# A hybrid trunk on one core: block inverses issued in another rhythm beside two projections, one scaling moved to ScalarE, and a gate in one operation

## The chip, the cores and the metric

The kernel runs on one core of one Trainium2 chip. The metric is the device time of one execution in microseconds (us). A core has TensorE (matrix products, PE in the profile; its weight loads are listed as PEld), VectorE (DVE), ScalarE (ACT), GpSimd (POOL), SyncE (SP, which here only issues transfers) and 16 DMA engines. Each engine runs its own instructions in one fixed order and waits by semaphores for the others. PSUM is the small memory that TensorE writes to.

## The reference, cut to what matters

The trunk has two layers over 1024 tokens of width 1024, batch 1: one RWKV-7 layer, one differential attention layer, a gated input embedding after each, and a last norm. The change lies in the first layer:

```
xm = h + dx * mu                          # one mix for each of r, k, v and gate
r, k, v, gate = xm_i @ w_in[i]            # four projections, 1024 x 1024 each
kk = k * k_k / |k * k_k| per head ;  b = kk * a
for t in tokens:                          # 16 heads, a state of 64 x 64 each
    sa    = state @ kk_t
    state = state * w_t - sa b_t^T + v_t k_t^T
    y_t   = state @ r_t
y = groupnorm(y) + bonus
h = h + (y * silu(gate)) @ w_out
```

## The kernel before, in words

**The recurrence in chunks.** The scan over tokens is done in 16 chunks of 64 tokens. Inside a chunk the steps depend on each other through a unit lower triangular matrix of 64 x 64 per head, which has to be inverted. With 16 chunks and 16 heads there are 256 such matrices. They don't depend on the state, so they are inverted ahead of the chain of chunks, and the results lie in the tiles `ti`, which the chain's products `u` read.

**Four quarters.** The inverses are made for four chunks at a time, in quarters 0 to 3, by three generators. They issue a piece of work at each `next` and then `yield`, so that the pieces can be written between other work:

- `inv_pb` (from L507): for each of four chunks it loads `bb` and `kk` and multiplies them on TensorE into two PSUM tiles `pb` (32 products of 64 x 64). Each `pb` times a factor per token, head and chunk (`rn`) goes to a part of the tile `nq` (L531). The PSUM tag "aux" has two buffers, so `pb` of the next chunk can only start when both have been read.
- `inv_diag` (from L534): it transposes the four 32 x 32 blocks on the diagonals of `nq` into `nb` (L542), inverts 32 x 32 triangles for all matrices at once in 31 steps of two VectorE operations each (L558, L560, tiles `tm` and `tb`), and transposes the result into `ea` (L570) and `ti` (L575). The copies `prhs` and `ti` (L574, L578) are ScalarE's.
- `inv_merge` (from L581): it makes the block below the diagonal from the two inverted ones by two rounds of 64 small products (`pg`, then `po`, L593), with ScalarE's copies `pairs` and `prhs` between (L603, L604) and behind.

A quarter's `inv_merge` runs beside the next quarter's `inv_pb` and `inv_diag`; `inv_steps` takes turns between the two generators.

**Where they are written.** The pieces are interleaved with two projections, by calls of `tick`. The v projection is 32 tiles of 24 products of 256 columns (L657 to L661), each tile copied to `vst` on ScalarE and stored to DRAM (L664). The gate projection (`dense_T`, L691) is 16 tiles of 24 products of 512 columns; its `ev_g` makes the sigmoid by a tanh on ScalarE and two VectorE operations (L645, L646). Every product is done in three parts (L75 to L77), high times high, high times low and low times high, from tiles that `split` makes. The gate's own operand `xm` is made during the last v tiles by `make_half` (`xmt` on ScalarE, L228, and VectorE, L229, then a cast and a subtraction on GpSimd). From the 48th `gtick` on everything that is left of the inverses is issued at once, and then the first pieces of `stage1` (transposes `kbt`, products `pm`, `prt`) for the first chunk of the chain.

**What sets the order.** The Tile scheduler takes the program and sets a static order per engine from the dependences and its own estimate of times; what is written earlier goes first where both could start. Only the products in one `turns` list are tied to each other. So an instruction may stand ahead of work that was written before it.

**Names.** A tile's number tells its place: `pb41` is chunk 4, half 1; `nq1`, `nb1`, `ea0`, `ti0` belong to quarters 1, 1, 0, 0; `v17` is column quarter 1 and token block 7 of v; `d360` is the projection with index 3 (gate), tile 6, half 0; `wv...h` and `...l` are high and low parts of weights.

Of the kernel before, what the change touches and what calls it, by code (L numbers as in the profile page):

```python
# [36 lines left out]
@with_exitstack  # L37
def trunk(ctx: ExitStack, tc: tile.TileContext, A, out):
    nc = tc.nc
    V, S, G, T = nc.vector, nc.scalar, nc.gpsimd, nc.tensor  # L40

    cp = ctx.enter_context(tc.tile_pool(name="const", bufs=1, reuse_waits="tile"))
    dp = ctx.enter_context(tc.tile_pool(name="scratch", bufs=1, space=DRAM))
# [26 lines left out]
    def split(hi, lo, src, lo_eng=None):  # L70
        S.activation(hi, src, AF.Copy)
        (lo_eng or G).tensor_tensor(out=lo, in0=src, in1=hi.bitcast(F32), op=ALU.subtract)

    def mm3(ps, ah, al, bh, bl, start, stop):
        T.matmul(ps, lhsT=ah, rhs=bh, start=start, stop=False)  # L75
# [117 lines left out]
    with NB("ab") as ab, NP("psab") as pp:  # L193
# [306 lines left out]
        def inv4(tag, nm):  # L500
            return iv.tile([P, 32, 32], F32, tag=tag, name=nm, bufs=1)

        Y1, Y2 = 3, 2
        nqs = {}
        ivt = []

        def inv_pb(q):  # L507

            nq = iv.tile([P, 4, 2, 4, L], F32, tag="nq", name=f"nq{q}", bufs=1)
            nqs[q] = nq.rearrange("p c h j l -> p (c h j) l")  # L510
            for cc in range(4):
                c = 4 * q + cc
                bb = iv.tile([P, KT, L], F32, tag="bb", name=f"bb{c}", bufs=2)
                kk = iv.tile([P, KT, L], F32, tag="kk", name=f"kk{c}", bufs=2)
                for t, src in ((bb, kb_d), (kk, kkr_d)):
                    for st in range(2):
                        js = slice(4 * st, 4 * st + 4)
                        nc.sync.dma_start(out=t[:, js], in_=src[js, :, c, st].rearrange("j p l -> p j l"))

                pb = [pp.tile([P, 4, L], F32, tag="aux", name=f"pb{c}{h}", bufs=2) for h in range(2)]  # L520
                ms = []
                for p_ in range(4):
                    for st in (1, 0):
                        o = 64 * st
                        for h in (1, 0):
                            hs_ = slice(h * 64, h * 64 + 64)
                            ms.append(T.matmul(pb[h][o:o + 64, p_], lhsT=bb[hs_, 4 * st + p_],
                                               rhs=kk[hs_, 4 * st + p_], start=True, stop=True))
                turns(ms)
                for h in range(2):  # L530
                    V.tensor_tensor(out=nq[:, cc, h], in0=pb[h],  # L531
                                    in1=rn[:, c, h].unsqueeze(2).to_broadcast([P, 4, L]), op=ALU.mult)
                    yield

        def inv_diag(q):

            nqf = nqs[q]
            nb = inv4("nb", f"nb{q}")
            for st in range(2):
                for b in range(2):  # L540
                    r0 = 64 * st + 32 * b
                    V.transpose(nb[r0:r0 + 32],  # L542
                                nqf[r0:r0 + 32, :, 32 * b:32 * b + 32].rearrange("p h t -> p t h"))
                yield
            tb = inv4("tb", f"tb{q}")
            G.memset(tb, 0.0)
            G.memset(tb.rearrange("p a b -> p (a b)")[:, 0::33], 1.0)
            ti = tis[q]
            tm = iv.tile([P, 256], F32, tag="tm", name=f"tm{q}", bufs=1)
            if not ivt:  # L550

                ivt[:] = iv.tile([P, 16, 32], F32, name="prhs"), iv.tile([P, 16, L], F32, name="pairs")
                G.memset(ivt[1], 0.0)
            prhs, pairs = ivt
            for j in range(31):
                w, n = j + 1, 31 - j
                tv = tm[:, 0:n * w].rearrange("p (n w) -> p n w", w=w)
                V.tensor_tensor(out=tv, in0=tb[:, j:j + 1, 0:w].to_broadcast([P, n, w]),  # L558
                                in1=nb[:, j + 1:32, j:j + 1].to_broadcast([P, n, w]), op=ALU.mult)
                V.tensor_tensor(out=tb[:, j + 1:32, 0:w], in0=tb[:, j + 1:32, 0:w], in1=tv, op=ALU.add)  # L560
                if j % 4 == 3:
                    yield
                if j == 28:
                    for st in range(2):
                        o = 64 * st
                        for y in range(2):
                            S.copy(pairs[o + 32 * y:o + 32 * y + 32, :, 32 * y:32 * y + 32],
                                   nqf[o:o + 32, 16 * y:16 * y + 16, 32:64])
            ea = inv4("ea", f"ea{q}")
            V.transpose(ea.rearrange("p h s -> p s h"), tb.rearrange("p t s -> p s t"))  # L570
            for st in range(2):
                o = 64 * st
                for y in range(2):
                    S.copy(prhs[o + 32 * y:o + 32 * y + 32], ea[o:o + 32, 16 * y:16 * y + 16])  # L574
            V.transpose(ti[:, :, 0:32].rearrange("p h t -> p t h"), tb)  # L575
            for st in range(2):
                r = slice(64 * st + 32, 64 * st + 64)
                S.copy(ti[r, :, 32:64], ti[r, :, 0:32])  # L578
                G.memset(ti[r, :, 0:32], 0.0)

        def inv_merge(q):  # L581

# [16 lines left out]
            for st in range(2):  # L599
# [3 lines left out]
                    S.copy(pairs[r, :, 32 * y:32 * y + 32], pg[st][r])  # L603
                    S.copy(prhs[r], ti[o + 32:o + 64, hs_, 32:64])  # L604
                yield
            for _ in range(Y2 + 1):
                yield
            po = products("po")
            yield
# [4 lines left out]
                yield  # L614

        def inv_steps():
            for q in range(5):
                def first():
                    if q < 4:
                        yield from inv_pb(q)  # L620
                        yield from inv_diag(q)
                a, b = first(), inv_merge(q - 1) if q else iter(())
                alive = True
                while alive:
                    alive = False
                    for g in (a, b):
                        if next(g, g) is not g:
                            alive = True
                            yield

        bg = inv_steps()

        due = [0.0]
        TV, TG = 1.0, 2.0

        def tick(n):
            due[0] += n
            while due[0] >= 1.0:
                due[0] -= 1.0
                next(bg, None)  # L640

        def ev_g(j, hf, ps):
            e = ab.tile([P, 512], F32, tag="xmt", name=f"ge{j}{hf}", bufs=3)
            S.activation(e, ps, AF.Tanh, scale=0.5)
            V.tensor_scalar(out=e, in0=e, scalar1=0.5, scalar2=0.5, op0=ALU.mult, op1=ALU.add)  # L645
            V.tensor_tensor(out=e, in0=ps, in1=e, op=ALU.mult)  # L646
            nc.scalar.dma_start(out=sg_d[j, :, half(hf)], in_=e)


        new = [None, None]  # L650
        for q in range(4):
            wv = [wload(f"wv{q}{k2}", A["wv"][q, k2].rearrange("p k c -> p (k c)")) for k2 in range(2)]
# [20 lines left out]
        def gtick():  # L673

            npt[0] += 1
            if npt[0] < 48:
                tick(TG)
            elif npt[0] == 48:
                tick(1000)
                iv_cm.__exit__(None, None, None)  # L680
                cm = early["cm"] = tc.tile_pool(name="early", bufs=1, reuse_waits="tile", side="right")
                e = early["co"] = cm.__enter__()
# [8 lines left out]
        dense_T(3, A["wT"][2], new, ev_g, None, gtick)  # L691
        while first:
            first.pop(0)()

    nslot = [0]

# [119 lines left out]
    with NB("d") as d, NP("psco") as pp:  # L816
# [119 lines left out]
        def d1_pieces(i):  # L936
# [38 lines left out]
            def turn(hf):  # L975
# [6 lines left out]
                for q in range(4):  # L982
                    kt = hf * 4 + q
                    V.scalar_tensor_tensor(out=yg[:, kt], in0=ps[:, q], scalar=vec["ln_b"][:, kt:kt + 1],
                                           in1=yg[:, kt], op0=ALU.add, op1=ALU.mult)
                split(gh[:, hs], gl[:, hs], yg[:, hs], V)

            def mms(hf, k0):
                gh, gl = w["gh"], w["gl"]
# [645 lines left out]
```

## Time and profile before

| | us |
|---|---|
| median of 3 runs | 1830.32 (1828.99 to 1832.56) |
| the profiled execution | 1828.3 |
| its span | 1826.5 |
| TensorE busy | 1684.7 (92%) |
| VectorE busy | 1350.9 (74%) |
| ScalarE busy | 760.4 (42%) |
| GpSimd busy | 634.5 (35%) |

The mean granted TensorE clock of the span is 0.963. The chain that ended last is 51% TensorE and 10% VectorE. These are averages over projections, the recurrence, attention and the embedding; the change touches one stretch, from about 314 to 600 us, so most of what is read below is from there. A waiting engine is shown in the rows by what released it; times are us from the start of the span.

### The profile page before, as it was taken

The numbers are of one execution on the slowest core, as the hardware profiler recorded it, in microseconds if no ns is written. First come the engines' busy times: TensorE is split into PE (matmuls) and PEld (weight loads), VectorE is DVE, ScalarE is ACT, GpSimd is POOL, SyncE is SP. The second block draws the span as 40 slices with busy tenths as digits, with TensorE's granted clock in tenths as the row PEclk, the third lists the DMA queues.
The fourth block names the chain that finished last, engine by engine and source line by source line (L and its number), as shares of the span: only waits on it lengthen the run. The fifth ranks groups of instructions, "written<-read, shape, count | busy, mean of one in ns | idle before, by whom it ended". The sixth has DMA issues, their size and how long they took to land.

```text
span 1826.5 us, 30473 instructions
## 1 busy us (share of the span) xinstructions
PE 1684.7 (92%) x11320; PEld 1397.6 (77%) x11320; DVE 1350.9 (74%) x3083; ACT 760.4 (42%) x1594; POOL 634.5 (35%) x705
## 2 busy tenths in 40 slices
PE   6899999898897988898899999899999999999998
PEld 5677778887676877777678878788888888777786
DVE  7878954698994687666766747887877878856665
ACT  6566543346344332223333434444444444544332
POOL 4436644224324355455310333323323323311200
PEclk9999999998998989999999999999999999999999
DMA  7125444434225534444243411101101101431121
GB/s 267 41 61 166 129 106 109 125 102 119 73 67 186 186 127 127 122 129 131 97 172 128 132 51 39 54 7 56 56 7 56 53 10 56 154 99 34 58 93 69
DMA packets 164401, 175.97 MB, mean 96 GB/s; under 512 B 74845, under 2 KB 127837, under 8 KB 164254
## 3 DMA queue, kind: packets, MB, share of 16 engines
q1 hardware_dynamic: 161950, 169.84, 30.2%
q10 hardware_dynamic: 2304, 4.20, 0.6%
q8 instruction: 89, 1.46, 0.4%
q14 instruction: 58, 0.48, 0.1%
HBM read 124.19 MB, written 49.81 MB: 95 GB/s over the span
## 4 chain that ended last, share of the span: by engine, by line
PE 51%; DVE 10%; ACT 2%; issue 1%; DMA 0%; POOL 0%; ACTq 0%; DVEq 0%
PE qkv L75 6%; PE qkv L76 6%; PE qkv L77 6%; PE av L1359 3%; PE sc L1319 2%; PE sc L1320 2%; PE fg L75 2%; PE fg L76 2%; PE fg L77 2%; PE op L75 2%; PE op L77 2%; PE op L76 2%; PE do L75 1%; PE pg L76 1%; PE pg L77 1%; PE do L76 1%
## 5 line engine op out<-in xcount | busy, mean ns | idle before, releaser
L1329 ACT ACTIVATE e<-sc,mx 128x256 f32<-128x256 f32 (+7 forms) x128 | 94.0, 738 | 111.0 <-DVE mx L1326 60.0
L1273 POOL TENSOR_TENSOR rp<-rp,rq 128x128 f32<-128x128 f32 x64 | 34.8, 543 | 237.6 <-DVE rq L1268 189.7
L1359 PE MATMUL av<-vh,aT 128*128 128x128 f32 x576 | 81.1, 280 | 6.3 <-DVE aT L1355 6.3
L1359 PEld LDWEIGHTS av<-vh,aT 128*128 128x128 f32 x576 | 75.6, 195 | 12.8 <-DVE aT L1355 8.9
L1325 DVE TENSOR_REDUCE mxs<-sc 128x1 f32<-128x128 f32 (+6 forms) x112 | 74.2, 682 | 0.5
L1319 PE MATMUL sc<-k,q 128*128 128x512 f32 (+2 forms) x192 | 71.5, 379 | 2.2 <-ACT e L1329 2.2
L229 DVE SCALAR_TENSOR_TENSOR xmt<-hT,cB,xmt 128x512 f32<-128x512 f32 x64 | 63.5, 1012 | 6.6 <-ACT xmt L228 6.3
L1320 PE MATMUL sc<-k,q 128*128 128x512 f32 (+2 forms) x192 | 64.8, 348 | 0.0
L1361 ACT ACTIVATE o<-av,r 128x128 f32<-128x128 f32 x64 | 23.5, 367 | 88.4 <-PE av L1359 88.4
L875 POOL TENSOR_TENSOR spl<-state,plast 64x256 f32<-64x256 f32 x60 | 41.4, 690 | 49.6 <-DVE state L910 42.7
L1341 DVE SCALAR_TENSOR_TENSOR e<-e,r,e 128x128 f32<-128x128 f32 (+3 forms) x64 | 56.5, 883 | 1.2
L560 DVE TENSOR_TENSOR tb<-tb,tm 128x31 f32<-128x31 f32 (+15 forms) x124 | 53.9, 435 | 3.6
L558 DVE TENSOR_TENSOR tm<-tb,nb 128x31 f32<-128x31 f32 (+15 forms) x124 | 53.9, 434 | 3.6
L188 DVE TENSOR_TENSOR m<-pm,mmask 128x512 f32<-128x512 f32 x64 | 41.1, 682 | 20.0 <-PE pm L185 19.7
L1301 POOL CAST q<-q 64x128 fp32r<-64x128 f32 x128 | 38.5, 302 | 49.4 <-PE sc L1320 45.6
L1267 DVE TENSOR_TENSOR rp<-qkv,rc 128x256 f32<-128x256 f32 x64 | 27.1, 423 | 38.3 <-PE qkv L77 30.1
L1292 POOL CAST k<-k 64x256 fp32r<-64x256 f32 x64 | 26.1, 408 | 83.7 <-ACT k L1290 82.5
L185 PE MATMUL pm<-kkr,kb 64*128 64x128 f32 x512 | 50.8, 307 | 3.1 <-ACT kbn L176 2.2
L1355 DVE COPY aT<-at 128x512 f32<-128x512 f32 (+2 forms) x96 | 52.0, 550 | 1.1 <-PE at L1353 0.4
L185 PEld LDWEIGHTS pm<-kkr,kb 64*128 64x128 f32 x512 | 40.4, 203 | 12.9 <-issue 6.0
L1353 PE MATMUL at<-ident,e 128*128 128x128 f32 x288 | 47.4, 277 | 2.8 <-DVE e L1341 2.3
L923 ACT COPY y<-xy 64x512 f32<-64x512 f32 x32 | 18.6, 580 | 71.4 <-PE xy L916 71.0
(1180 smaller groups left out, 6001.5 us busy)
## 6 DMA issues: line engine op xcount, KB each, us to landing
pp_d<-ppo SPq DMA_DIRECT2D x32, 256.0 KB, 2.3
kb_d<-kb SPq DMA_DIRECT2D x16, 512.0 KB, 2.6
kkr<-kkr_d SPq DMA_DIRECT2D x32, 256.0 KB, 3.2
kb<-kb_d SPq DMA_DIRECT2D x32, 256.0 KB, 3.3
x<-in_x SPq DMA_DIRECT2D x8, 512.0 KB, 5.5
kkr_d<-ep SPq DMA_DIRECT2D x16, 256.0 KB, 2.6
kkr_d<-rt SPq DMA_DIRECT2D x16, 256.0 KB, 2.6
bb<-kb_d SPq DMA_DIRECT2D x32, 128.0 KB, 2.6
```

The costliest lines, as they stand in the source:

```text
L75: T.matmul(ps, lhsT=ah, rhs=bh, start=start, stop=False)
L76: T.matmul(ps, lhsT=ah, rhs=bl, start=False, stop=False)
L77: T.matmul(ps, lhsT=al, rhs=bh, start=False, stop=stop)
L185: ms.append(T.matmul(pm[h][:, p_], lhsT=kb[hs, p_], rhs=kkr[hs, p_], start=True, stop=True))
L229: V.scalar_tensor_tensor(out=t, in0=hT[:, kt, half(hf)], scalar=cB[:, g, kt:kt + 1], in1=t, op0=ALU.mult, op1=ALU.add)
L558: V.tensor_tensor(out=tv, in0=tb[:, j:j + 1, 0:w].to_broadcast([P, n, w]), in1=nb[:, j + 1:32, j:j + 1].to_broadcast([P, n, w]), op=ALU.mult)
L1319: T.matmul(ps[:, b0:b1], lhsT=q1[:, m, ts_], rhs=k1[:, m, b0:b1], start=True, stop=False)
L1320: T.matmul(ps[:, b0:b1], lhsT=q0[i % 2][:, m], rhs=k2[:, b0:b1], start=False, stop=True)
L1325: V.tensor_reduce(out=seed, in_=ps[:, 0:n - P], axis=AX.X, op=ALU.min)
L1329: S.activation(e[:, 0:n], ps[:, 0:n], AF.Exp, scale=-1.0, bias=mx, accum_out=l_[:, m:m + 1])
L1341: V.scalar_tensor_tensor(out=es[0][:, 0:n], in0=es[1][:, 0:n], scalar=r[:, 1:2], in1=es[0][:, 0:n], op0=ALU.mult, op1=ALU.add)
L1359: T.matmul(po, lhsT=aT[kb // 4][:, kb % 4], rhs=c["vh"][:, kb], start=(kb == 0), stop=(kb == i))
```

## The change

- All four engines are reached through a small wrapper. While `pin` is set for TensorE, from the first v tile to the end of the gate projection and the first `stage1` pieces, each of its instructions keeps the order in which it is written; the scheduler still orders the other engines. (The wrapper is line 50 of the changed kernel, and all its instructions bear that line.)
- The scaling of `pb` by `rn` goes from two VectorE operations of 128 x 256 per chunk to eight ScalarE operations of 128 x 64, each with its factor per partition as a pointer operand.
- The four transposes into `nb`, each over 32 partitions, become one over all 128 and two over 32 (the first writes something into the two ranges that the other two then overwrite).
- A `yield` tells a cost, by its size VectorE's time for the piece, and `tick` goes on issuing until the due time is used up. `inv_steps` moves both generators on at once. The constants for v and gate (TV, TG), the distances of `inv_merge` (Y1, Y2) and the last `gtick` (51 instead of 48) change with it.
- The gate's two VectorE operations become one: (tanh + 1) x product, which is twice what it was; the factor 0.5 is put back in `split_half`, which takes the place of `split` for the mixer's output (16 calls in the chain).

```
+    class Engine:
+        def __init__(self, eng):
+            self.eng, self.pin = eng, False
+        def __getattr__(self, nm):
+            f = getattr(self.eng, nm)
+            def g(*a, **k):
+                r = f(*a, **k)
+                if self.pin:
+                    tc.keep_in_program_order(r)
+                return r
+            return g
+    V, S, G, T = engines = [Engine(e) for e in (nc.vector, nc.scalar, nc.gpsimd, nc.tensor)]
...
+    def split_half(hi, lo, src):
+        S.activation(hi, src, AF.Copy, scale=0.5)
+        V.scalar_tensor_tensor(out=lo, in0=src, scalar=0.5, in1=hi.bitcast(F32), op0=ALU.mult, op1=ALU.subtract)
...
-        Y1, Y2 = 3, 2
+        Y1, Y2 = 4, 1
...
                 for h in range(2):
-                    V.tensor_tensor(out=nq[:, cc, h], in0=pb[h],
-                                    in1=rn[:, c, h].unsqueeze(2).to_broadcast([P, 4, L]), op=ALU.mult)
-                    yield
+                    for j in range(4):
+                        S.activation(nq[:, cc, h, j], pb[h][:, j], AF.Copy, scale=rn[:, c, h, j:j + 1])
+                yield 1.0
...
+            V.transpose(nb, nqf[:, :, 0:32].rearrange("p h t -> p t h"))
+            yield 2.2
             for st in range(2):
-                for b in range(2):
-                    r0 = 64 * st + 32 * b
-                    V.transpose(nb[r0:r0 + 32],
-                                nqf[r0:r0 + 32, :, 32 * b:32 * b + 32].rearrange("p h t -> p t h"))
-                yield
+                r = slice(64 * st + 32, 64 * st + 64)
+                V.transpose(nb[r], nqf[r, :, 32:64].rearrange("p h t -> p t h"))
+                yield 2.0
...
                 if j % 4 == 3:
-                    yield
+                    yield 3.5
...
+            yield 2.6
             ea = inv4("ea", f"ea{q}")
...
+            yield 4.2
...
-            for _ in range(Y2 + 1):
+            for _ in range(Y2):
                 yield
             po = products("po")
...
                 a, b = first(), inv_merge(q - 1) if q else iter(())
-                alive = True
-                while alive:
-                    alive = False
-                    for g in (a, b):
-                        if next(g, g) is not g:
-                            alive = True
-                            yield
+                while True:
+                    ca, cb = next(a, None), next(b, 0)
+                    if ca is None and cb == 0:
+                        break
+                    yield ca or 2.0
...
-        TV, TG = 1.0, 2.0
+        TV, TG = 1.75, 1.6
         def tick(n):
             due[0] += n
-            while due[0] >= 1.0:
-                due[0] -= 1.0
-                next(bg, None)
+            while due[0] > 0.0:
+                due[0] -= next(bg, 1e9)
...
             S.activation(e, ps, AF.Tanh, scale=0.5)
-            V.tensor_scalar(out=e, in0=e, scalar1=0.5, scalar2=0.5, op0=ALU.mult, op1=ALU.add)
-            V.tensor_tensor(out=e, in0=ps, in1=e, op=ALU.mult)
+            V.scalar_tensor_tensor(out=e, in0=e, scalar=1.0, in1=ps, op0=ALU.add, op1=ALU.mult)
...
+        T.pin = True
         new = [None, None]
         for q in range(4):
...
-            if npt[0] < 48:
+            if npt[0] < 51:
                 tick(TG)
-            elif npt[0] == 48:
-                tick(1000)
+            elif npt[0] == 51:
+                tick(1e6)
...
         while first:
             first.pop(0)()
+        T.pin = False
...
-                split(gh[:, hs], gl[:, hs], yg[:, hs], V)
+                split_half(gh[:, hs], gl[:, hs], yg[:, hs])
```

What it does to the order shows at three places. The first is VectorE between quarter 0 and quarter 1, before; a row is line, operation, output, inputs and shape, and x4 stands for four of a kind in a row:

```order
L531 TENSOR_TENSOR nq1_3258<-pb61_3476,rn_75 128x256
L560 TENSOR_TENSOR tb0_3077<-tb0_3077,tm0_3080 128x6x26
L531 TENSOR_TENSOR nq1_3258<-pb60_3475,rn_75 128x256
...
L558 TENSOR_TENSOR tm0_3080<-tb0_3077,nb0_3032 128x31
L560 TENSOR_TENSOR tb0_3077<-tb0_3077,tm0_3080 128x31
L570 STREAM_TRANSPOSE ea0_3247<-tb0_3077 128x32x32
L575 STREAM_TRANSPOSE ti0_2684<-tb0_3077 128x32x32
L531 TENSOR_TENSOR nq1_3258<-pb71_3566,rn_75 128x256
L531 TENSOR_TENSOR nq1_3258<-pb70_3565,rn_75 128x256
L542 STREAM_TRANSPOSE nb1_3641<-nq1_3258 32x1024 x4
```

The same place after:

```order
L50 TENSOR_TENSOR tm0_3020<-tb0_3017,nb0_2972 128x31
L50 TENSOR_TENSOR tb0_3017<-tb0_3017,tm0_3020 128x31
L50 STREAM_TRANSPOSE ea0_3326<-tb0_3017 128x32x32
L50 STREAM_TRANSPOSE ti0_2684<-tb0_3017 128x32x32
L50 STREAM_TRANSPOSE nb1_3549<-nq1_3365 128x1024
L50 STREAM_TRANSPOSE nb1_3549<-nq1_3365 32x1024 x2
```

The scalings of quarter 1 stood among the last steps of quarter 0; now VectorE has none of them, and its next instruction behind `ti0` reads the whole of `nq1`. The second place is ScalarE there, after:

```order
L50 COPY prhs_3021<-ea0_3326 32x512 x4
L50 ACTIVATE nq1_3365<-pb41_3373,rn_75 128x64
L50 ACTIVATE nq1_3365<-pb40_3372,rn_75 128x64 x4
L50 ACTIVATE nq1_3365<-pb41_3373,rn_75 128x64 x3
L50 COPY ti0_2684<-ti0_2684 32x32x32 x2
L50 COPY vst17_3410<-v17_3352 128x256
L50 ACTIVATE wv30h_3883<-wv30r_3881 128x1024
L50 ACTIVATE nq1_3365<-pb51_3420,rn_75 128x64 x4
L50 ACTIVATE nq1_3365<-pb50_3419,rn_75 128x64 x4
```

Where before only `prhs`, `ti` and `vst` copies followed `ea0`, the scalings of chunks 4 to 7 now stand, the first of them behind the four copies that read `ea0`. The third place is TensorE where chunks 4 to 7 are multiplied, before:

```order
L527 MATMUL pb41_3266<-kk4_3260,bb4_3259 64x64
...
L527 MATMUL pb51_3348<-kk5_3342,bb5_3341 64x64
...
L527 MATMUL pb61_3476<-kk6_3470,bb6_3469 64x64
...
L527 MATMUL pb71_3566<-kk7_3560,bb7_3559 64x64
```

and after, first product of each group with the product ahead of it:

```order
L50 MATMUL v17_3352<-wv10h_3085,xm2_3_1l_2645 128x256
L50 MATMUL pb41_3373<-kk4_3367,bb4_3366 64x64
...
L50 MATMUL v17_3352<-wv11h_3091,xm2_7_1l_2673 128x256
L50 MATMUL pb51_3420<-kk5_3414,bb5_3413 64x64
...
L50 MATMUL pb61_3452<-kk6_3446,bb6_3445 64x64
...
L50 MATMUL v20_3489<-wv20h_3479,xm2_3_0l_2531 128x256
L50 MATMUL pb71_3509<-kk7_3503,bb7_3502 64x64
```

Before, 48 v products stood between two chunks. Now `pb4` comes later in v (tile `v17`), and the four follow one another with 12, 0 and 12 v products between.

## Rows read from the trace of the kernel before

**Rows 1.** Windows: length; PE, PEld, DVE, ACT, POOL busy (instructions); PEclk; DMA share; GB/s

```profile
314.40:449.00 134.60, 120.53 (x1441) 115.52 (x1439) 108.86 (x185) 59.66 (x103) 39.86 (x27) 0.92 0.42 110
449.00:571.00 122.00, 112.08 (x739) 87.53 (x740) 102.60 (x183) 54.99 (x89) 36.36 (x25) 0.93 0.32 99
571.00:597.20 26.20, 16.29 (x112) 13.10 (x109) 14.79 (x15) 10.68 (x14) 16.44 (x15) 0.67 0.66 210
```

**Rows 2.** Waits of PE, 314 to 571 us: releaser, us, count, longest

```profile
PE pb L527 <- DVE nq L531: 5.6, 4, 3.5
...
PE pg L593 <- ACT prhs L574: 4.9, 4, 3.1
```

**Rows 3.** Timeline of DVE: start, us, instruction

```profile
347.31 8.27 DVE L542 STREAM_TRANSPOSE nb<-nq 32x1024 f32<-32x1024 f32 x4
...
384.66 2.16 DVE L570 STREAM_TRANSPOSE ea<-tb 128x1024 f32<-128x1024 f32 x1
...
546.80 2.20 DVE L570 STREAM_TRANSPOSE ea<-tb 128x1024 f32<-128x1024 f32 x1
```

**Rows 4.** Timeline of PE: start, us, instruction [wait ahead]

```profile
389.40 2.15 PE L593 MATMUL pg<-prhs,pairs 64*64 64x32 f32 x64 [3.12 <-ACT prhs L574]
...
489.35 1.23 PE L527 MATMUL pb<-kk,bb 64*64 64x64 f32 x32 [3.53 <-DVE nq L531]
...
565.14 0.39 PE L75 MATMUL d<-xm_1h,w_7h 128*128 128x512 f32 x1
565.37 0.39 PE L76 MATMUL d<-xm_1l,w_7h 128*128 128x512 f32 x1
...
570.74 0.60 PE L175 MATMUL kbt<-ident,kbp 128*128 128x128 f32 x4
...
577.83 2.67 PE L185 MATMUL pm<-kkr,kb 64*128 64x128 f32 x16 [0.37 <-DVE m L188]
...
597.18 1.15 PE L890 MATMUL u<-x,ti 64*64 64x64 f32 x32
```

**Rows 5.** Groups by line, 344 to 552 us: busy, mean ns | idle before

```profile
L531 DVE TENSOR_TENSOR nq<-pb,rn 128x256 f32<-128x256 f32 x26 | 9.8, 412 | 3.5 <-PE pb L527 3.5
...
L645 DVE TENSOR_SCALAR ge<-ge 128x512 f32<-128x512 f32 x12 | 6.0, 503 | 0.0
...
L229 DVE SCALAR_TENSOR_TENSOR xmt<-hT,cB,xmt 128x512 f32<-128x512 f32 x16 | 14.1, 892 | 6.1 <-ACT xmt L228 6.1
...
L228 ACT ACTIVATE xmt<-hT,cA 128x512 f32<-128x512 f32 x16 | 11.0, 716 | 7.6 <-DMA v_d<-vst 4.6 <-POOL xm_1l L72 1.7 <-DVE xm_0l L72 1.2
```

**Rows 6.** Windows of tile tm on DVE, the 31 steps of each quarter

```profile
355.60:384.66 29.06, 25.40 (x62) 1.00 0.57 159
397.28:425.40 28.12, 25.44 (x62) 1.00 0.34 100
455.56:500.10 44.54, 29.40 (x62) 0.92 0.25 82
512.30:546.80 34.50, 27.48 (x62) 0.90 0.25 84
```

**Rows 7.** Timeline of ACT, small operations elsewhere in the span

```profile
1122.39 0.37 ACT L1361 ACTIVATE o<-av,r 128x128 f32<-128x128 f32 x1 [2.26 <-PE av L1359]
...
1122.95 0.27 ACT L1269 COPY vh<-qkv 128x128 f32<-128x128 f32 x1 [0.19 <-DVE rq L1268]
1123.11 0.28 ACT L1271 ACTIVATE sg<-qkv 128x128 f32<-128x128 f32 x1
...
1690.85 0.62 ACT L1419 ACTIVATE g<-o,sub 128x128 fp32r<-128x128 f32 x2
```

**Rows 8.** Timeline of ACT, copies in the stretch

```profile
333.31 0.37 ACT L664 COPY vst<-v 128x256 f32<-128x256 f32 x1 [0.73 <-DMA v_d<-vst]
...
386.85 2.50 ACT L574 COPY prhs<-ea 32x512 f32<-32x512 f32 x4 [6.36 <-DVE ea L570]
389.38 2.11 ACT L578 COPY ti<-ti 32x1024 f32<-32x1024 f32 x2
```

More of the change, by code (lines that the diff above doesn't have):

```diff
@@ L39, in trunk @@
     nc = tc.nc
-    V, S, G, T = nc.vector, nc.scalar, nc.gpsimd, nc.tensor
+    class Engine:
[10 more added lines that the diff above has]
+    V, S, G, T = engines = [Engine(e) for e in (nc.vector, nc.scalar, nc.gpsimd, nc.tensor)]
     cp = ctx.enter_context(tc.tile_pool(name="const", bufs=1, reuse_waits="tile"))
```

## The prediction, made before the changed kernel was run

> **What bounds the kernel now.** I read the windows first. The change lies in one stretch, 314.4 to 571 us, where TensorE multiplies for v and then for the gate while VectorE inverts 128 blocks in four quarters; the static order of all five engines is the same ahead of it and again from the first chunks of the chain on. In this stretch both big engines look full: TensorE is busy 120.5 of 134.6 us beside v and 112.1 of 122 us beside the gate, VectorE 108.9 and 102.6; ScalarE is under half [rows 1]. So busy shares do not name the bound, and I went to TensorE's waits: 5.6 us for `nq` to leave PSUM, 4.9 us for `prhs` before `pg` [rows 2]. Both stand behind the inverses. VectorE's own timeline shows a chain: first `nb` transposes at 347.3 us, last `ea` at 546.8 us, so 549.0 us at its end [rows 3]. What the stretch costs is how soon that last `ea` ends, and what TensorE has left then: 48.2 us from there to the first `u` product of the chain at 597.18 us [rows 4]. After that nothing is changed but the 16 halvings of `split_half`, which move a factor from one operand to another of two operations that stay; I cost them at nothing (a bound either way: under 0.1 us on each).
>
> **What the change takes from VectorE.** Per quarter a transposing step fewer: four took 8.27 us [rows 3], three take 6.1 us (the one over 128 partitions counted as `ea` with its 2.16 us, the others as a quarter of 8.27 us). The 26 `nq` products of the stretch, 412 ns each, go to ScalarE; beside the steps they lengthen VectorE's line by about 0.67 us a pair, 8 us for the three quarters behind the first. Gate: 12 operations of 503 ns vanish within the stretch [rows 5], 9 of them ahead of the last `ea`. In all some 8 + 8 + 4 = 20 us less work on the chain's engine. The 31 steps of a quarter stay: 25.40, 25.44, 29.40, 27.48 us [rows 6], each plus 62 gaps of 0.03 us, 27.3, 27.3, 31.3, 29.4 us. The longer ones are those beside POOL's subtractions, which go on.
>
> **What it adds between two quarters.** In the order of after, `pb` of the next quarter is written behind the whole of `inv_diag`, and VectorE has no step left to run while `nq` is made: `ea`, `ti`, then at once `nb` of the next quarter, which reads all of `nq`. On ScalarE the first `nq` stands behind the four `prhs` copies, and these wait for `ea`. With two PSUM buffers, each `pb` of a chunk waits for the eight scalings of the chunk before it. So a chain of hand-overs opens where before `nq` of the next quarter had been made in the shadow of the steps.
>
> The price of eight scalings has no row. Two 128 x 128 operations without a pointer operand start 0.16 us apart; two with one take 0.62 us, of which the last is 0.37 us, so 0.25 us apart [rows 7]. 64 columns less save 0.05 us (half of the 0.10 us between 0.27 us for 128 columns and 0.37 us for 256 [rows 7, 8]): 7 x 0.20 + 0.32 = 1.75 us. Below: no cost for the pointer, 7 x 0.11 + 0.22 = 1.0 us. Above: no overlap, 8 x 0.37 = 3.0 us. I take 1.75 us, by the pointer pair, the nearest row. The Trainium skill, "ScalarE: Activation LUTs", section "What ACT_TABLE_LOAD costs", gives 186 ns + 0.833 ns per column, about 93 ns more for each pointer operand, and about 93 ns of overlap back to back. By the page, eight would be an estimated 2.0 us, and the sum below 3 us later; the trace's 0.09 us between the two pairs agrees with the pointer's price.
>
> - From the end of `ea` 0 to `nb` 1: `prhs` 2.50 us [rows 8]; scalings 1.75; two `ti` copies 2.11 [rows 8], a `vst` 0.37 and a cast of 1024 columns at 1.0 (half of the two `ti`), within which chunk 5 is multiplied, 3.45; scalings 1.75; `pb` after an idle stretch 1.1 (1.23 in its row against 0.7 in a busy stretch [rows 4]); twelve v products at half clock 2.6 (as long as six gate products), which hide the next scalings; `pb` 0.9; scalings 1.75. Sum 15.8 us.
> - To `nb` 2: `prhs`, `ti`, `vst` 5.0; scalings 1.75; two `xmt` at 0.72 [rows 5] and a `vst` 1.8; scalings 1.75; two casts of 512 columns at 0.5 (half of the one of 1024) and an `xmt` 1.7; scalings 1.75; two `xmt` and three such casts 2.95; eight scalings with an `xmt` among them, and the hand-over to it, 2.95. Sum 19.7 us, in which eight of the sixteen `xmt` products hide.
> - To `nb` 3: `prhs`, `ti` 4.6; a cast 1.0 and a gate's tanh 0.5; scalings 1.75; `pb` 1.1; scalings 1.75; `pb` 1.1; six gate products at half clock 2.8 (6 x 2 x 0.2325 [rows 4]); `pb` 1.1; scalings 1.75. Sum 17.5 us.
>
> Each hides `ti`'s transpose, 2 us. What TensorE could do meanwhile is written behind the waiting `pb`, and now stays there.
>
> **The sum along VectorE.** First `nb`: the fourth `vst` ends at 333.7 us [rows 8]; from there four batches of scalings 7.0, three `pb` 2.4 and 1.2 for the loads of chunks 2 and 3 give 344.3 us, against 347.3. Then quarter 0: 6.1 + 27.3 + 2.2 = 35.6, `ea` ends at 379.9; plus 15.8 is 395.7; quarter 1 to 431.3; plus 19.7 is 451.0; quarter 2 with ten `xmt` products at 0.75 us (of 892 ns in the mean with their waits [rows 5]), one subtraction 0.7 and three gate operations at 0.7 to 500.9; plus 17.5 is 518.4; quarter 3, 6.1 + 29.4 + 2.2 and five gate operations 3.5, to 559.6 us. Before it was 549.0 us: 10.6 us later, 20 us less work and 3 us at the start against some 53 us of hand-overs, of which before had about 20 us as its own waits, `nq` and `xmt` there.
>
> **TensorE behind it.** The last `pb` ends at 516.6 us; `pg` 2.15 [rows 4] and 1.5 for a half clock after the waits; 174 gate products at a mean of 0.2325 us (the two shown start 0.23 us apart), 40.4, and `po` 2.1: it reaches the last `pg` at 562.7 us, `prhs` is there at 562.1. Then `pg`, 24 products, `po`: 572.5 us. Before, 26 products and the first chunk's `kbt`, `pm`, `prt` followed; now 78, with those among them: 18.1 + 4.5 (two `kbt` at 0.60, two `pm` of eight at half of 2.67 [rows 4], two `prt` counted at 0.3) + 0.6 for waits = 595.7 us. From there to the first `u` the order has one `kbt`, eight `pm`, `xy`, `prt`, `kbt`, `pm`, and the copies of x, all at full clock: 7.6 us. Before, the granted clock was 0.67 from 571 to 597.2 us and TensorE busy 16.3 of 26.2 us [rows 1]; that loss goes, since gate products fill it. The first `u` comes at 603.3 us instead of 597.2: +6.1 us.
>
> The profiled execution took 1828.3 us, of which its span is 1826.5 us; 1828.3 + 6.1 = 1834.4 us. The median of the runs is 2.0 us above it, so I forecast 1836 us. A difference under 0.2%, 3.7 us, counts as none here.
>
> **Rivals.**
> 1. Faster: the hand-overs are shorter than summed and VectorE's 20 us come through. The prices at their lower end: 1.0 us for eight scalings, on the path some 12 times, -9 us; `pb` at 0.7 us in seven places, -3 us; no half clock in the three spots, -4 us. All three, 16 us: 1820 us. For it: ScalarE was busy under half of the stretch [rows 1], and no row shows a 64-column scaling. Against it: the order puts each behind a wait, so its idle time is of no use there. The Trainium skill, "Perfetto Trace Analysis", section "Optimizing Scalar/DVE Operations", says that with VectorE saturated, work that ScalarE can do may go there. By that rule the change gains what it takes away, and the time is at or below this rival's; the trace agrees as to VectorE's load, and not that ScalarE is free at that moment.
> 2. Slower, beyond the forecast: TensorE in written order pays for its waits with its clock. After an idle 3.5 us `pb` took 1.23 us [rows 4]. By my sum TensorE waits about 8 us ahead of chunk 5, 4 us ahead of chunk 9, and over 10 us ahead of chunk 13. Beside v it has that time to spare; from chunk 15 on it is itself the path. Were the stretch behind chunk 15 at half clock for 14 us, 7 us are lost instead of 1.5, and the third gate tile, which can't be passed any more while `xm` of its half is made, takes up to 5 us: 1846 us. It decides once TensorE reaches the last `pg` over 3 us behind `prhs`.
> 3. No change: VectorE's savings and the hand-overs cancel; 5 us less in the three sums than I count, 1831 us. Nothing in the rows excludes it, and it lies inside the forecast's own range.
>
> **Chances.** The forecast with its own range, 1829 to 1842 us, has 0.47: of this 0.27 slower, 0.15 the same, 0.05 faster. The first rival 0.30: 0.28 faster, 0.02 the same. The second 0.21, slower. The third is part of the first two and adds 0.02 the same. Together 0.33 faster, 0.19 the same, 0.48 slower. For the range, the upper price of the scalings (3.0 us, +15 us) and the second rival reach past 1850 us, the first goes down to 1820 and somewhat under it if loads and casts are hidden too: 1811 to 1852 us leaves out about 2 in 10.
>
> **What will show it.** VectorE idle for 12 to 16 us ahead of each of the three later `nb`, released by ScalarE's `nq`; `nq` itself at 0.20 us a piece; the last `ea` ending near 560 us and the first `u` near 603 us; TensorE's waits at `pb` of chunks 5, 9 and 13 instead of at `pg` and `po`; a granted clock near 1 behind the gate. I am wrong if VectorE's idle stretches are half as long, since then the last `ea` ends ahead of 549 us; or if the kernel gains behind the last `ea`, in less time than 44 us from it to the first `u`.

## The result: 1854.55 us, 1.3% slower, and the profile after

| | before | after |
|---|---|---|
| median, us | 1830.51 (4 runs) | 1854.55 (4 runs, 1850.87 to 1859.28) |
| ratio to before, 95% interval | | 1.0132 (1.0105 to 1.0159) |
| profiled execution; its span, us | 1828.3; 1826.5 | 1859.28; 1856.3 |
| first v product to first `u`, us | 282.7 | 303.0 |
| first to last `u` of the chain (16 chunks), us | 305.5 | 312.7 |
| TensorE at half clock in these two, us | 54.6 and 34.1 | 81.9 and 54.6 |

The forecast was 1836 us, 1811 to 1852: the direction held, the size did not, and the time lies above the range. The windows show where (columns as in [rows 1], whose three lines are the same stages before; from the first v product to the first gate product, to the last gate product, to the first `u`), after:

```profile
316.48:472.07 155.59, 123.15 (x1410) 118.25 (x1408) 110.23 (x176) 83.21 (x205) 42.12 (x29) 0.86 0.38 99
472.07:606.30 134.23, 120.70 (x813) 92.48 (x812) 84.03 (x148) 60.65 (x116) 36.44 (x28) 0.87 0.28 85
606.30:619.47 13.17, 11.20 (x101) 9.25 (x101) 7.63 (x9) 6.84 (x9) 10.64 (x11) 0.87 0.76 247
```

Stage v takes 21 us more, at a clock of 0.86 instead of 0.92, and stage gate 12 us more. The last part gains 13 us: TensorE idles for 2.0 us there instead of 9.9. Cut at the end of the last `pb` (chunk 15), the same stretch before (two lines) and after (two lines) shows on which side the loss is:

```profile
314.44:490.57 176.13, 155.35 (x1648) 140.29 (x1646) 148.97 (x250) 79.80 (x136) 61.54 (x39) 0.92 0.40 108
490.57:597.18 106.61, 93.49 (x641) 75.85 (x640) 77.21 (x134) 45.54 (x68) 31.07 (x27) 0.87 0.39 125
316.48:523.88 207.40, 163.93 (x1655) 146.25 (x1653) 147.60 (x238) 110.36 (x262) 62.35 (x43) 0.83 0.35 94
523.88:619.47 95.59, 91.12 (x674) 73.72 (x671) 54.28 (x95) 40.34 (x67) 26.86 (x25) 0.95 0.34 109
```

Up to the last `pb` 31.3 us are lost, and behind it 11.0 are regained. The waits of TensorE and VectorE in the stretch, after (releaser: us, times, longest):

```profile
PE pb L50 <- ACT nq L50: 32.3, 9, 8.6
PE po L50 <- ACT prhs L50: 4.4, 2, 2.4
...
DVE nb L50 <- ACT nq L50: 38.6, 3, 14.8
```

Against [rows 2], 5.6 us of waiting for `nq` have become 32.3. The hand-over behind quarter 0 on ScalarE (start, duration), which was to be 15.8 us:

```profile
384.89 2.50 ACT L50 COPY prhs<-ea 32x512 f32<-32x512 f32 x4 [6.04 <-DVE ea L50]
387.41 1.75 ACT L50 ACTIVATE nq<-pb,rn 128x64 f32<-128x64 f32 x8
389.18 2.11 ACT L50 COPY ti<-ti 32x1024 f32<-32x1024 f32 x2
391.31 0.37 ACT L50 COPY vst<-v 128x256 f32<-128x256 f32 x1
391.71 1.06 ACT L50 ACTIVATE wv30h<-wv30r 128x1024 fp32r<-128x1024 f32 x1
392.67 1.73 ACT L50 ACTIVATE nq<-pb,rn 128x64 f32<-128x64 f32 x8
395.68 1.75 ACT L50 ACTIVATE nq<-pb,rn 128x64 f32<-128x64 f32 x8 [1.28 <-PE pb L50]
399.65 1.75 ACT L50 ACTIVATE nq<-pb,rn 128x64 f32<-128x64 f32 x8 [2.22 <-PE pb L50]
```

The same stretch on VectorE, with the last `ea` of the four quarters:

```profile
382.86 2.00 DVE L50 STREAM_TRANSPOSE ea<-tb 128x1024 f32<-128x1024 f32 x1
...
401.43 6.05 DVE L50 STREAM_TRANSPOSE nb<-nq 128x1024 f32<-128x1024 f32 x3 [14.80 <-ACT nq L50]
...
562.04 2.23 DVE L50 STREAM_TRANSPOSE ea<-tb 128x1024 f32<-128x1024 f32 x1
```

And on TensorE, `pb` of chunks 4 to 7, the last `po` and the first `u`:

```profile
377.69 0.69 PE L50 MATMUL pb<-kk,bb 64*64 64x64 f32 x32
...
388.59 1.84 PE L50 MATMUL pb<-kk,bb 64*64 64x64 f32 x32 [8.60 <-ACT nq L50]
393.64 0.48 PE L50 MATMUL pb<-kk,bb 64*64 64x64 f32 x2 [3.20 <-ACT nq L50]
...
398.47 1.13 PE L50 MATMUL pb<-kk,bb 64*64 64x64 f32 x32
...
578.32 3.62 PE L50 MATMUL po<-prhs,pairs 64*64 64x32 f32 x64 [2.05 <-ACT prhs L50]
...
607.72 0.66 PE L50 MATMUL kbt<-ident,kbp 128*128 128x128 f32 x4 [1.41 <-DVE ge L50]
...
619.47 0.74 PE L50 MATMUL u<-x,ti 64*64 64x64 f32 x18
```

Eight scalings take 1.75 us, as estimated. TensorE stands still for 8.6 and 3.2 us ahead of `pb` and then works at half clock: the `pb` at 398.47 us, ahead of which it didn't wait, takes 1.13 us instead of 0.69. (The 1.84 us at 388.59 are not the clock alone: two of the 32 products are early, and the others start 0.4 us later.)

### The profile page after: what moved, and what is told of

The parts are those of the page before. It is cut to its first block, busy times and chain, and to the rows that moved or that the text cites. A ratio compares the mean times of both kernels' runs of the same rounds, so it can differ in the third digit from the quotient of the medians.

```text
span 1856.3 us, 30576 instructions
## 1 busy us (share of the span) xinstructions
PE 1695.6 (91%) x11320; PEld 1403.6 (76%) x11320; DVE 1325.2 (71%) x3031; ACT 788.5 (42%) x1722; POOL 631.8 (34%) x705
## 4 chain that ended last, share of the span: by engine, by line
PE 53%; DVE 10%; ACT 2%; issue 2%; DMA 1%; SPq 0%; POOL 0%; ACTq 0%; DVEq 0%; POOLq 0%
PE qkv L50 18%; PE fg L50 5%; PE pg L50 4%; PE do L50 4%; PE op L50 4%; PE sc L50 3%; PE av L50 3%; PE xy L50 2%; DVE ost L50 2%; PE at L50 1%; PE pps L50 1%; PE pm L50 1%; DVE gst L50 1%; PE u L50 1%; DVE aT L50 1%
## 5 line engine op out<-in xcount | busy, mean ns | idle before, releaser
L50 POOL TENSOR_TENSOR rp<-rp,rq 128x128 f32<-128x128 f32 x128 | 61.8, 503 | 240.1 <-DVE rq L50 191.9
L50 PE MATMUL sc<-k,q 128*128 128x512 f32 (+2 forms) x384 | 88.8, 362 | 2.2 <-ACT e L50 2.2
L50 PE MATMUL pg<-pwg,ph 128*128 128x512 f32 x224 | 73.1, 406 | 0.2 <-ACT ph L50 0.2
L50 PE MATMUL do<-dwo,oh 128*128 128x512 f32 x224 | 71.7, 401 | 0.8 <-DVE h L50 0.6
L50 PEld LDWEIGHTS sc<-k,q 128*128 128x128 f32 x384 | 63.4, 190 | 11.4 <-ACT e L50 3.1
L50 DVE STREAM_TRANSPOSE nb<-nq 32x1024 f32<-32x1024 f32 (+1 forms) x12 | 24.3, 2024 | 38.8 <-ACT nq L50 38.6
```

The costliest lines, as they stand in the source:

```text
L50: r = f(*a, **k)
```

## The experiments

Times are medians; "stretch" is first v product to first `u`, "chain" first to last `u`, both of the run's profile. "Hand-overs" is the sum, over three quarters, from the end of `ea` to the start of the next `nb`: 24.1 us before (2.4, 19.8, 1.9) and 53.6 us after (16.6, 19.4, 17.6).

**One edit taken back, or one made alone.** The edits of the first, the second and the third run:

```
e1, changed kernel:
-        T.pin = True
+        T.pin = False
e2, changed kernel (e3: the kernel before with the reverse):
-                    for j in range(4):
-                        S.activation(nq[:, cc, h, j], pb[h][:, j], AF.Copy, scale=rn[:, c, h, j:j + 1])
+                    V.tensor_tensor(out=nq[:, cc, h], in0=pb[h],
+                                    in1=rn[:, c, h].unsqueeze(2).to_broadcast([P, 4, L]), op=ALU.mult)
```

> The changed kernel, but TensorE is not held to the written order; all else as changed. Theory A (the written order costs: TensorE stands idle at pb for 32 us and at half clock behind, and can't pull products forward): about 1833 us, TensorE's waits at pb of nq under 8 us in the stretch. Rival B (the scalings on ScalarE cost, behind the prhs copies): VectorE's three hand-overs stay near 16 to 19 us and the time stays at 1847 to 1855 us. Rival C (the pace: pb comes only when the quarter before is issued to its end): hand-overs stay as under B, TensorE fills them, 1840 to 1847 us.

Measured 1839.17 us, ratio 1.0046 (1.0023 to 1.0068); stretch 284.7, chain 317.2 us; hand-overs 34.8 us. 15.4 of the 24 us go away with the written order; theory A is nearest, though 6 us short of its time. Waits of TensorE in this run:

```profile
PE pb L50 <- ACT nq L50: 7.6, 3, 3.5
PE d L50 <- ACT vst L50: 6.6, 1, 6.6
PE pg L50 <- ACT prhs L50: 5.7, 2, 2.9
```

> The changed kernel, but nq is made by VectorE as before, two operations per chunk. Theory A (written order): pb stands in the same places, the time stays at 1848 to 1856 us. Rival B (scalings on ScalarE): each chunk's hand-over falls from 1.75 us or more to 0.9 us and no longer waits for prhs, the hand-overs fall from about 17 to about 9 us, three times, so 1832 us within 5. Rival C (pace): hand-overs still 9 to 12 us, 1838 to 1846 us.

Measured 1847.25 us, ratio 1.0096 (1.0064 to 1.0128); stretch 296.7, chain 305.0. Hand-overs 51.8 us: their sum hardly shrinks, so rival B falls as a cause of them; the time lies just below what theory A said. Other waits took the place of the scalings, first the load of the next chunk's `kk`, which also starts late (issued at 386.16 us for the `pb` at 389.40):

```profile
PE pb L50 <- DMA kk<-kkr_d: 14.4, 5, 3.9
PE pb L50 <- DVE nq L50: 8.3, 3, 5.7
```

> The kernel before with one edit: nq by ScalarE in eight operations per chunk. Rival B (scalings cost wherever they stand): 1838 to 1850 us. Theories A and C (scalings are harmless where pb is spread over the quarter before): 1826 to 1833 us.

Measured 1834.31 us, ratio 1.0027 (1.0014 to 1.0040); stretch 286.8, chain 311.4. Between the two: the scalings on ScalarE cost 4.8 us where nothing else is changed (the stretch is 4.1 us longer).

The fourth is the kernel before with the new transposes and the new gate of the diff above, and nothing else.

> The kernel before with the two savings on VectorE alone: three transposes into nb instead of four, and the gate in one operation with the half in split_half. If VectorE's chain sets the end of the stretch, as the prediction has it, 4 x 2.1 + 9 x 0.5 = 13 us less on it and 1818 to 1824 us; if TensorE's products set it, 1828 to 1832 us.

Measured 1830.40 us, ratio 0.9999 (0.9989 to 1.0009). The last `ea` ends 9 us sooner and the stretch is 276.7 us, 6.0 less than before, yet the time is the same. In the profiles 2.7 us are given back in the chain (308.2 us), 2.3 behind it, and v starts 1.6 us later.

**Another place for `pb`.**

```
e5, changed kernel (e6: also 45 for 51 in gtick):
-        Y1, Y2 = 4, 1
+        Y1, Y2 = 1, 1
...
-                if j == 28:
+                if q < 3 and j in (18, 21, 24, 27):
+                    pbs.setdefault(q + 1, inv_pb(q + 1)).__next__()
+                if j == 16:
...
-                        yield from inv_pb(q)
+                        yield from pbs.get(q) or inv_pb(q)
```

> The changed kernel with one thing moved: pb and the scalings of a quarter are written at steps 18, 21, 24 and 27 of the quarter before (the copies of nq into pairs go from step 28 to step 16, Y1 from 4 to 1), TensorE still in written order, scalings still on ScalarE. Theory A (the four pb in 24 products behind the end of a quarter are the cost): the three hand-overs on VectorE fall from 16 to 19 us to under 3 us, TensorE's waits at pb from 32 us to under 10 us, and the time to 1815 to 1835 us. Rival (written order costs whatever stands where): 1842 us or more.

Measured 1841.89 us, ratio 1.0072 (1.0057 to 1.0087): the expectation of theory A missed. VectorE gained what was wanted (hand-overs 26.8 us, last `ea` ends at 532.0 us, 17 us sooner than before), but TensorE did not: its idle stretches over 0.1 us add up to 46.5 us, against 47.6 after, the last gate product ends at 591.4 us against 570.9 before, and the first `u` comes at 609.3. Its waits:

```profile
PE pb L50 <- ACT nq L50: 25.3, 5, 8.4
PE d L50 <- ACT vst L50: 9.0, 1, 9.0
```

The wait for `vst` is new, and TensorE idles for as long as after. Yet the time is 12.7 us below the changed kernel's: TensorE is at half clock for 61.4 us of the stretch instead of 81.9, the stretch is 9 us shorter and the chain 10. So the place of `pb` is worth at most half of the loss (the chain's order, of which more below, is not held here); the idle time was only moved.

> As the run before, and the last of the inverses and the first pieces of the chain are written from the 45th gtick on instead of the 51st (36 gate products sooner). If what stands between the last po and the first u is a chain of loads, transposes and products that gate products can hide, the first u comes 5 to 9 us sooner than in the run before; if TensorE is full up to there, no change within 2 us.

Measured 1838.30 us, ratio 1.0050 (1.0033 to 1.0066); the first `u` only 0.4 us sooner, as the second case said. TensorE isn't quite full up to there: from the last gate product to the first `u` it is busy 14.06 of 17.95 us.

The seventh takes back both edits of e1 and e2; the eighth sets the pin in the kernel before, with the wrapper of the changed one:

```
e8, kernel before:
+        T.pin = True
         new = [None, None]
...
         while first:
             first.pop(0)()
+        T.pin = False
```

> The changed kernel with TensorE free and nq on VectorE, so that of its changes to the inverses the pace, the transposes and the gate are left. If written order (15 us by the first experiment) and scalings (7 us by the second) add up: 1832 us within 4. If they are one hand-over that either of the two shortens: 1836 to 1840 us. If the pace by itself costs nothing, it is at 1830 us.

Measured 1838.10 us, ratio 1.0043 (1.0031 to 1.0055). The stretch is 278.0 us, 4.7 shorter than before, and hand-overs are 25.4 us, nearly the 24.1 of before; but the chain has 316.1 us. So the time lies in the second case's range for another reason than that case gives.

> The kernel before with TensorE held to the written order of its v and gate projections, at the old pace, scalings on VectorE. If written order costs by itself: 1845 us or more. If it costs only where the four pb stand together: 1828 to 1836 us. Its pace is not in units of VectorE's time, so pg and po may be written too early and TensorE wait there: then over 1850 us, with the waits at pg and po and not at pb.

Measured 1877.69 us, ratio 1.0264 (1.0249 to 1.0279), as the last of the three cases said: the wait is at `pg`, written too early for that pace.

```profile
PE pg L49 <- ACT prhs L49: 61.4, 4, 25.8
PE d L49 <- ACT vst L49: 9.1, 1, 9.1
```

**The chain's order.** e4 and e7 lose behind the first `u` much or all of what they gain ahead of it. I compared the static order there: it is not the same, though my prediction said so. The scheduler moves the products that fill the chain (`pps`, `op`) against those of the chunks; by the traces before and after, the sequence of products on TensorE differs in chunks 0 to 4 and 8 to 10. From `u` of chunk 0 on:

```
before: u x32; pm x14; pps x12; s x32; xy x32
after:  u x32; pps x4; kbt x4; pm x2; pps x6; s x32; xy x32
```

So I built kernels whose five engines are held, from the first instruction written behind the gate to the end, to the order that the scheduler gave the kernel before (names shortened):

```
+    ins = list(nc.cur_bb.bb.instructions)[mark:]
+    for eng, places in CHAIN_ORDER.items():
+        mine = [x for x in ins if str(x.engine) == eng]
+        row = [mine[k] for k in places]
+        for a, b in zip(row, row[1:]):
+            tc.add_manual_dep(b, a.name, DependencyInfo(NoSync, DATA), reason="order")
```

> The changed kernel, but behind the gate all five engines are held to the order that the scheduler gave the kernel before there (from the chain's first chunk to the end). Theory S (the scheduler wrote the chain anew and that order costs the 7 us by which the chain was longer in the profile): first u 22 us later as in the changed kernel, the chain from first to last u 304 to 308 us instead of 312.7, the time 1845 to 1850 us. Rival N (the 7 us are the state in which the chain starts, or chance): 1852 to 1857 us.

Measured 1857.21 us, ratio 1.0156 (1.0139 to 1.0173): no gain; the first `u` is at 622.8 us, the chain 311.4 us. For the changed kernel as it is, rival N stands. In its chain TensorE has the order, the number of products, the busy time (270.74 us) and the granted clock (0.94) of before; the 5.9 us by which it is longer are idle time.

> The kernel before with three transposes and the gate in one operation (as in the fourth experiment), and behind the gate the order of before. Theory S: the 6 us that the stretch gained there come through, 1822 to 1826 us. Rival N, or if the chain is bound by something that doesn't start sooner: 1829 to 1831 us again.

Measured 1818.08 us, ratio 0.9940 (0.9922 to 0.9957): 12.3 us less than e4, which differs in the chain's order alone, faster than both kernels, and below what theory S said. Stretch 276.4, chain 305.2 us. (The profile, of the slowest of four runs, shows 6 us of it.)

> The changed kernel with TensorE free, nq on VectorE (as in the seventh experiment), and behind the gate the order of before. The stretch was 4.7 us shorter there than before, the chain 10.6 us longer. Theory S: chain 304 to 308 us, 1825 to 1830 us. Rival N: 1836 to 1839 us again.

Measured 1824.09 us, ratio 0.9967 (0.9956 to 0.9979), 14.0 us less than e7, as theory S said within 1 us. The windows of the chain, e7:

```profile
594.60:910.80 316.20, 275.00 (x3244) 230.56 (x3243) 215.20 (x436) 87.05 (x139) 151.89 (x159) 0.92 0.41 127
```

and e11, with the same products, at a better clock:

```profile
595.50:901.00 305.50, 269.36 (x3244) 227.32 (x3244) 213.56 (x423) 85.31 (x136) 151.85 (x159) 0.95 0.42 130
```

> The changed kernel once more, for a second profile: how much of the stretch (303.0 us from the first v product to the first u) and of the chain (312.7 us) is chance. If both are set by the order: within 2 us of these. If the chain's length is chance: 305 to 318 us.

Measured 1859.05 us (one run): stretch 301.8, chain 313.9 us. As far as two profiles can tell, both lengths belong to the kernel and not to chance.

**The edits with the chain's order held.** The last five have the edits of the runs above, and the order of before behind the gate.

> The changed kernel with TensorE free and nq on ScalarE, chain in the order of before; against the ninth experiment only the written order is gone, against the eleventh only nq moved. If the written order is most of the cost (the stretch was 18 us shorter without it): 1830 to 1836 us. If the hand-over on ScalarE is: 1842 us or more.

Measured 1831.98 us, ratio 1.0011 (0.9998 to 1.0024): the written order is most of the cost.

> The changed kernel with nq on VectorE, TensorE in written order, chain in the order of before. The stretch was 6.3 us shorter than in the changed kernel: 1847 to 1853 us if the price of nq on ScalarE is what it was there; under 1840 us if the hand-over was the main cost after all.

Measured 1846.14 us, ratio 1.0083 (1.0060 to 1.0106): near the first case.

> The kernel before with nq on ScalarE alone, chain in the order of before. The stretch was 4.1 us longer: 1832 to 1836 us. If the scalings cost only through the chain's new order: 1828 to 1831 us.

Measured 1833.00 us, ratio 1.0018 (1.0001 to 1.0034): the first case, just clear of no difference.

> The kernel before with the gate in one operation (and the half in split_half) alone, chain in the order of before; with both savings it took 1818 us. By VectorE's time ahead of the last ea (9 x 0.5 us of 12.9) a third of the 11.6 us comes from the gate: 1825 to 1827 us. If the transposes do nothing: 1817 to 1820 us.

Measured 1828.19 us, ratio 0.9984 (0.9973 to 0.9996): less than expected of the gate.

> The kernel before with three transposes into nb instead of four, nothing else, chain in the order of before. If the savings add up: 1819 to 1821 us. If what the transposes take from VectorE's chain is all that counts (4 x 2.1 us, of which the stretch passes on some 5): 1822 to 1826 us, and the rest of e10 comes only of both together.

Measured 1821.87 us, ratio 0.9958 (0.9944 to 0.9972): 7.9 us from the transposes, 1.6 from the gate, 11.6 from both.

With the chain's order held, one edit behind the other, each row from the medians:

| step | us | from, to |
|---|---|---|
| transposes and gate | -11.6 | 1829.71, e10 1818.08 |
| pace (yields, TV, TG, Y1, Y2, flush) | +6.0 | e10, e11 1824.09 |
| `nq` on ScalarE | +7.9 | e11, e13 1831.98 |
| written order on TensorE | +25.2 | e13, e9 1857.21 |

Taken in the other order, the last two steps are 22.1 us for the written order (e11 to e14) and 11.1 for the scalings (e14 to e9). The stretch lengths, without that hold, rank the steps alike: -6.0 (e4), +1.3 (e7), +6.7 (e1), +18.3 (after), in sum the 20.3 us. The written order is the main cost.

## Why the prediction was wrong

**What held.** VectorE's chain did matter: an estimated 8.4 us less of transposes gave 7.9 us (e17). The price of eight scalings was 1.75 us; that it fits to the hundredth is luck, since it came from rows of other sizes. By the rate of the Trainium skill ("ScalarE: Activation LUTs", section "What ACT_TABLE_LOAD costs") it was an estimated 2.0 us; the trace puts the scalings closer together than the page. The hand-overs were forecast at 53.0 us and measured 53.6. The last `ea` ended at 564.3 us, 4.7 later than forecast, of which 2.0 are the later start of v. The first rival (faster) was wrong: e10 is the gain that it spoke of, and it needs neither the moved scalings nor the written order.

**The step that failed: "TensorE behind it", and "after that nothing is changed".** The forecast for the profiled execution was 1834.4 us, measured 1859.3. The 24.9 us divide, term by term:

| term of the sum | forecast | measured | us |
|---|---|---|---|
| start of v | 314.4 | 316.5 | 2.0 |
| end of the last `pb`, from the start of v | 202.2 | 207.4 | 5.2 |
| 174 gate products and one `pg`, `po` to the last `pg` | 46.1 | 44.6 | -1.5 |
| last `pg` to the end of `po` | 9.8 | 13.5 | 3.7 |
| 78 gate products with `kbt`, `pm`, `prt` | 23.2 | 24.4 | 1.2 |
| last gate product to first `u` | 7.6 | 13.2 | 5.5 |
| chain | 305.5 | 312.7 | 7.1 |
| behind the last `u`, and outside the span | 925.6 | 927.2 | 1.6 |

The sum saw most of the delay up to the last `pb`: 202.2 us from the start of v against 176.1 before, measured 207.4. It failed behind it: from the last `pb` to the first `u` TensorE was to regain 19.9 us (106.6 to 86.7) and regained 11.0 (95.6). The `po` waited 2.0 us for `prhs` and ran at half clock, 3.62 us instead of 2.1. Behind the gate I had left out `pps`, the wait of 1.41 us for the gate's last `ge` and a slower clock (0.87). Each is small; I read them as TensorE without a choice of what to do next, but the runs show that cost only as a whole (e13 to e9), not term by term. On TensorE's own path I priced half clock at 1.5 us; measured, the stretch has 27 us more at half clock than before and 14 us more idle time. Both come from ahead of the last `pb`; behind it both fell. The second part, the chain, was put at nothing and measured 7.1 us; its cause stays open (below).

**The cause was put in the wrong place.** I took the hand-overs for a matter of ScalarE (scalings behind `prhs`). With the scalings back on VectorE they stayed at 51.8 us (e2), with TensorE free they fell to 34.8 (e1), with both to 25.4 (e7). It is `pb` that comes late; I read e1 as saying that this is because nothing may pass the products and waits ahead of it. What the scalings do cost by themselves is 7.9 us (e11 to e13) or 3.2 us (e15). The rule of the Trainium skill, "Perfetto Trace Analysis", section "Optimizing Scalar/DVE Operations", that a saturated VectorE may hand work to ScalarE, did not pay here: the runs give a loss in each surrounding (3.2, 7.9 and 11.1 us).

**The second rival.** "TensorE in written order pays for its waits with its clock" had a chance of 0.21 and said 1846 us, 8.6 too little. It was nearest, but not as it was written. Its sign was TensorE reaching the last `pg` over 3 us behind `prhs`; measured, `prhs` ended at 566.83 us and `pg` began at 568.45, 1.6 us behind. It put the half clock behind chunk 15 and said that beside v TensorE "has that time to spare"; but behind the last `pb` TensorE is at half clock for 10.2 us, against 26.9 before, and ahead of it for 71.7, against 27.7. Nor was the `pb` of 1.23 us after a wait [rows 4] much of a sign of the clock: in the kernel before, another took 1.12 us after a wait, at a granted clock of 1.00:

```profile
440.64 1.12 PE L527 MATMUL pb<-kk,bb 64*64 64x64 f32 x32 [1.61 <-DVE nq L531]
```

**The chain.** The sentence that the order is the same again from the first chunks on was wrong, and with it the price of nothing behind the first `u`. The order there cost 12.3 us (e4 against e10), 14.0 (e7, e11) and 7.2 (e1, e13), 1.3 in e3 and 1.1 in e2 (against e15 and e14), and for the changed kernel itself nothing (e9). So it does not explain the 7.1 us of the table: with the order of before the chain still took 5.9 us more than before, in idle time, and why is open. Why the order costs most where the first `u` comes early is open too: I did not find the single place in it. It also is why e4 seemed to show that VectorE's savings were worth nothing.

## What to carry to other kernels

Held to the written order, TensorE could not fill its waits with other work, and that cost 25.2 us here; moving the late work (e5) gave back 12.7 of the 24 us at most, while the idle time only moved. Before TensorE is pinned, add up its waits in the profile and ask what it did meanwhile. And where a scheduler plans the whole program by its own clock, an edit in one stage changes the order of the stages behind: compare the static order to the very end, and hold it fixed there when an edit is judged, or a good edit (e10, 0.6% faster than before) looks like no edit at all (e4).

## What the runs showed of the hardware

Eight operations of 128 x 64 with a factor per partition took 1.75 us back to back on ScalarE, 0.20 us apart. A transpose over 128 partitions takes no longer than one over 32: three with one such took 6.05 us, four of 32 took 8.27 [rows 3]. Where TensorE had stood idle from 380 us on, the granted clock was 0.50, the lower of its two levels (1.2 GHz), for all of this window:

```profile
383.77:400.83 17.06, 8.55 (x114) 7.52 (x115) 2.86 (x2) 12.29 (x38) 5.34 (x5) 0.50 0.44 113
```

The v products of 256 columns started 0.21 us apart in it and 0.12 us apart behind it:

```profile
396.20 0.41 PE L50 MATMUL v<-wv20h,xm_0l 128*128 128x256 f32 x1
396.42 0.41 PE L50 MATMUL v<-wv20h,xm_0h 128*128 128x256 f32 x1
...
401.04 0.28 PE L50 MATMUL v<-wv21l,xm_0h 128*128 128x256 f32 x1
401.15 0.28 PE L50 MATMUL v<-wv21h,xm_0l 128*128 128x256 f32 x1
```

A `pb` lasts longer after a wait at the higher clock too: 0.69 us without a wait (377.69), 1.12 after a wait at 1.00 (before, 440.64), and 1.13 without a wait at 0.50 (398.47).
